# GpSimd's element-wise work moved to VectorE in a two-block fp32 transformer kernel on Trainium2

## The chip, the cores and the metric

The kernel runs on one core of a Trainium2 chip. The metric is device time in microseconds for one execution; a version's time is the median of its runs. One execution more was recorded by the hardware profiler, and all rows below are from it. The engines are PE (TensorE: matrix products), DVE (VectorE: element-wise work), ACT (ScalarE: functions, scaled copies), POOL (GpSimd: here also element-wise work) and SP (transfers only).

## The reference

Two transformer blocks run one after the other on 512 rows of width 1024, all in fp32. The first is two layers of swiglu, a mixer (Fourier mix, dilated-window attention, differential attention) and a second swiglu. The second block is where most of the change lies:

```python
h = _rms_norm(x, g_mix_pre[l])
proj = h @ w_in[l]
aq, ak, av, dqkv, dgate, dalpha, dbeta = jnp.split(proj, IN_SPLITS, axis=-1)
...
attn_o = _window_attention(aq, ak, av, attn_sink[l]).astype(x.dtype)
dn_o = _gated_deltanet(dqkv, dgate, dalpha, dbeta, conv_w[l], a_log[l], dt_bias[l],
                       g_dn_out[l]).astype(x.dtype)
mix = jnp.concatenate([attn_o, dn_o], axis=-1) @ w_out[l]
x = x + _rms_norm(mix, g_mix_post[l])
c = _memory_cross_attention(_rms_norm(x, g_cross_pre[l]), _rms_norm(mem, g_mem[l]),
                            w_cq[l], w_ckv[l], w_co[l])
x = x + _rms_norm(c, g_cross_post[l])
f = _swiglu(_rms_norm(x, g_ffn_pre[l]), w_gate_up[l], w_down[l])
x = x + _rms_norm(f, g_ffn_post[l])
```

The gated deltanet takes queries, keys and values through a convolution of five taps, a silu and a norm, and then runs a recurrence over chunks, in both directions and for four heads.

## The kernel before

**Products.** Every large product is made of three: each operand is split into a high part (rounded to fp32r) and a low part (the rest), and high x high, high x low and low x high are summed. A weight slab is loaded by SP into `raw` (3 buffers); ACT writes the high part `whi` (5 buffers), and a subtraction writes the low part `wlo` (5 buffers). `split` does the subtraction on DVE. `split_w` is the same, but while `pool_w` is set (from the second block's mixer to the end of its cross attention) every second subtraction runs on POOL.

**Order of the work.** The program is written by tasks (Python generators) that `drive` runs by priority. Each recorded operation passes through `note`, which keeps an estimate of when each engine is free and when each tile is done; a task yields until the tile that it needs is due, and others are written in between. So an engine's order is fixed when the program is built, and an operation that moves to another engine changes the due times and with them the order of everything behind it. Work of low priority fills what would be waits: the gates and window projections, and `memory_proj` (priority 7), which multiplies the memory rows by K and V weights and sends six of its results to DRAM through POOL's queue.

**What POOL does before.** In the first block: the running sums of squares (`sq_pool`, L471), seven additions per norm. At the start of the second block's mixer: eight scalings of x by its norm (`final_norm`, L1258). In the mixer: four additions in each convolution of queries and values (`conv`), half of the weight splits, copies and products in `delta_k`; in `delta` the masks times beta and the scalings of values, keys and queries; and in `rope` the sine product and the sum. In the norms between mixer, cross attention and swiglu (`post_task`, `post_halves`): the odd chunks' scaling and sums. At the end: the gain of the last norm (`finish`). Fills (memset) and transfers too.

The convolution on POOL's path (queries, values) before: ACT makes three scaled copies, POOL adds two of them with a shift, DVE adds two taps, POOL adds the sum.

```python
if pool:
    zs = [self.g(), self.g()]
    for z, j in zip(zs, (0, 4)):
        nc.scalar.activation(z, t, AF.Copy, scale=wc(j))
    yield self.when(*zs)
    nc.gpsimd.tensor_tensor(zs[0][:, 0:S - 4], zs[0][:, 0:S - 4], zs[1][:, 4:S], ALU.add)
```

Of the kernel before, what the change touches and what calls it, by code (L numbers as in the profile page):

```python
# [135 lines left out]
class Net:  # L136
    def __init__(self, ctx, tc, ins, dump=None):
# [21 lines left out]
        self.pool_w = self.turn = False  # L159
# [146 lines left out]
    def split_w(self, src, hi, lo):  # L306

        self.nc.scalar.activation(hi, src, AF.Copy)
        self.turn = self.pool_w and not self.turn
        (self.nc.gpsimd if self.turn else self.nc.vector).tensor_tensor(lo, src, hi.bitcast(F32), ALU.subtract)  # L310
        return hi, lo

# [4 lines left out]
    def slab(self, src, kc, c, whole=False):  # L317
# [142 lines left out]
    def sq_pool(self, k, x):  # L460
# [9 lines left out]
        else:  # L470
            nc.gpsimd.tensor_tensor(self.acc[k], self.acc[k], q, ALU.add)  # L471

    def wide(self, srcs, us, first=4):
# [4 lines left out]
        for k in range(KC):  # L478
            if k % 4 == 0:
                self.lock, self.ahead = self.cur, True  # L480
                n = first if k == 0 else 4
                for j, src in enumerate(srcs):
# [5 lines left out]
                    for c in range(2):  # L488
                        hi = self.whi.tile([P, 4, P], F32R, tag="whi", name=self.nm("whi"))
                        lo = self.wlo.tile([P, 4, P], F32R, tag="wlo", name=self.nm("wlo"))  # L490
                        for k0 in range(0, 4, n):
                            self.split_w(raw[:, k0:k0 + n, c * P:(c + 1) * P], hi[:, k0:k0 + n], lo[:, k0:k0 + n])
# [744 lines left out]
    def final_norm(self, a1, a2):  # L1237
# [19 lines left out]
        for c in range(KC):  # L1257
            nc.gpsimd.tensor_tensor(self.x[c], self.x[c], r1b, ALU.mult)  # L1258
# [5 lines left out]
    def post_task(self, row, res, nxt, done):  # L1264
# [13 lines left out]
        for c in range(1, KC, 2):  # L1278
            nc.gpsimd.tensor_tensor(ms[c], ms[c], rb, ALU.mult)
# [55 lines left out]
    def post_halves(self, row, res, nxt, half, done):  # L1335
# [22 lines left out]
        def chunks(n, cs, p=None):  # L1358
            sl = slice(256 * n, 256 * n + 256)
            for c in cs:  # L1360
                if c % 2:
                    nc.gpsimd.tensor_tensor(ms[c][:, sl], ms[c][:, sl], rbs[n], ALU.mult)
            for c in cs:
# [14 lines left out]
                else:  # L1378
                    q = self.g(shape=[P, 256])
                    nc.scalar.activation(q, x, AF.Square)  # L1380
                    eng = nc.vector if c % 2 and n else nc.gpsimd
                    eng.tensor_tensor(self.acc[0][:, sl], self.acc[0][:, sl], q, ALU.add)
# [13 lines left out]
    def wide_halves(self, srcs):  # L1396
# [5 lines left out]
        for k in range(0, KC, 4):  # L1402
            w.append([])
            for j, src in enumerate(srcs):
# [3 lines left out]
                for c in range(2):  # L1408
# [5 lines left out]
                    w[-1].append(self.split_w(raw[:, :, c * P:(c + 1) * P], hi, lo))  # L1414
# [28 lines left out]
    def mixer2_task(self, after):  # L1443
# [4 lines left out]
        self.pool_w = True  # L1448
# [15 lines left out]
        def conv(p, x, h):  # L1464
# [8 lines left out]
            pool = x != 1  # L1473
            if pool:
                zs = [self.g(), self.g()]
                for z, j in zip(zs, (0, 4)):
                    nc.scalar.activation(z, t, AF.Copy, scale=wc(j))
                yield self.when(*zs)
                nc.gpsimd.tensor_tensor(zs[0][:, 0:S - 4], zs[0][:, 0:S - 4], zs[1][:, 4:S], ALU.add)
            yield self.when(y)  # L1480
            for j in (1, 3) if pool else (0, 1, 3, 4):
# [4 lines left out]
            if pool:  # L1486

                yield self.when(zs[0])
                nc.gpsimd.tensor_tensor(y[:, 2:S], y[:, 2:S], zs[0][:, 0:S - 2], ALU.add)
                nc.gpsimd.tensor_tensor(y[:, 0:2], y[:, 0:2], zs[1][:, 2:4], ALU.add)  # L1490
                yield self.when(y)
# [57 lines left out]
        self.pool_w = True  # L1549
# [124 lines left out]
    def delta_k(self, h, st):  # L1674
# [22 lines left out]
        for d in range(2):  # L1697
# [13 lines left out]
            nc.gpsimd.tensor_copy(self.kgs[c], v3(dt)[:, :, last])  # L1711
            self.dt[c] = dt
            lt = self.g()
            (nc.vector if d else nc.gpsimd).tensor_tensor(lt, dt, kkm, ALU.mult)
# [83 lines left out]
    def delta(self, h, d, oa, done, st):  # L1798
# [69 lines left out]
        nc.gpsimd.tensor_tensor(v3(rv), v3(rv), be3, ALU.mult)  # L1868
        nc.gpsimd.tensor_tensor(v3(kg), v3(kg), self.b3(self.kgs[c]), ALU.mult)
# [11 lines left out]
        nc.gpsimd.tensor_tensor(qgt, qgt, gq, ALU.mult)  # L1881
# [56 lines left out]
    def rope(self, t):  # L1938
# [8 lines left out]
        nc.gpsimd.tensor_tensor(o, o, self.sin, ALU.mult)  # L1947
        yield self.when(o)
        nc.gpsimd.tensor_tensor(t, t, o, ALU.add)
# [202 lines left out]
    def cross_task(self, after):  # L2152
# [53 lines left out]
        self.pool_w = False  # L2206
# [64 lines left out]
    def post_gain(self, gb):  # L2271
        nc, i = self.nc, self.i
        yield 100.0
        for h in range(2):
            nc.scalar.dma_start(gb[h], i["g_ffn_post_2"][0, h * S:(h + 1) * S].partition_broadcast(P))
            nc.gpsimd.tensor_scalar_mul(gb[h], gb[h], D ** 0.5)
# [61 lines left out]
    def finish(self, t, ps, ms, xn, gb, out):  # L2338
        nc = self.nc
        ss = self.small(2, "mss")  # L2340
        for h in range(2):
# [3 lines left out]
            nc.gpsimd.tensor_tensor(ms[h], ms[h], gb[h], ALU.mult)  # L2345
# [110 lines left out]
```

## Time and profile before

| what | value |
|---|---|
| median of 3 runs | 3448.17 us (3446.51 to 3451.38) |
| profiled execution, its own time | 3459.29 us |
| its span | 3457.5 us, 44625 instructions |
| PE busy | 3356.0 us (97%) |
| DVE busy | 1905.8 us (55%) |
| ACT busy | 1369.1 us (40%) |
| POOL busy | 337.6 us (10%) |
| mean granted clock of PE | 0.986 |

A busy time is the union of an engine's instructions. The granted clock is 1 when PE runs at 2.4 GHz and 0.5 at 1.2 GHz. The second block's mixer and cross attention lie between about 2506 and 3112 us.

### The profile page before, as it was taken

How to read it: one execution, taken by the hardware profiler on the slowest of the kernel's cores; microseconds unless marked ns; L12 is line 12 of the kernel's file. 1: busy time of each engine (PE TensorE's matmuls, PEld its weight loads, DVE VectorE, ACT ScalarE, POOL GpSimd, SP SyncE). 2: the span in 40 equal slices, each digit the busy share in tenths (PEclk: the TensorE clock that was granted, in tenths of full speed). 3: DMA queues.
4: the chain of work that ended last, by engine and by line, in shares of the span. 5: the costliest groups of instructions: out<-in, count | busy, mean ns of one | idle time of the engine just before them, and what ended most of it. 6: DMA issues, size and time to landing. Idle time of an engine off the chain costs nothing.

```text
span 3457.5 us, 44625 instructions
## 1 busy us (share of the span) xinstructions
PE 3356.0 (97%) x16759; PEld 2835.2 (82%) x16759; DVE 1905.8 (55%) x3644; ACT 1369.1 (40%) x2672; POOL 337.6 (10%) x325
## 2 busy tenths in 40 slices
PE   8999999999999999999999999999978889999998
PEld 7788888898888888888888987888867887788887
DVE  5444476656444444444767474545488764754344
ACT  4323445543332333234445443333354443443232
POOL 1000100000000000001000001000354433220001
PEclk9999999999999999999999999999999999999999
DMA  4533333435333333334333257333336453223232
GB/s 123 151 104 101 117 96 101 124 109 176 93 95 101 95 100 90 100 96 121 96 101 119 86 189 147 102 102 96 93 121 189 152 156 107 68 74 99 96 98 85
DMA packets 424422, 386.46 MB, mean 112 GB/s; under 512 B 31184, under 2 KB 379577, under 8 KB 424205
## 3 DMA queue, kind: packets, MB, share of 16 engines
q1 hardware_dynamic: 383584, 333.50, 32.2%
q10 hardware_dynamic: 40141, 48.54, 5.2%
q8 instruction: 131, 2.15, 0.3%
q0 software_dynamic: 480, 1.57, 0.1%
q14 instruction: 86, 0.70, 0.1%
HBM read 341.46 MB, written 37.88 MB: 110 GB/s over the span
## 4 chain that ended last, share of the span: by engine, by line
PE 90%; DVE 5%; DMA 2%; ACT 1%; issue 1%; POOL 0%; SPq 0%; ACTq 0%; DVEq 0%; POOLq 0%
PE ps L119 90%; DVE g L119 3%; DVE sm L119 1%; ACT g L119 1%; DVE wlo L119 0%; DMA raw<-in_w_ffn_gate 0%; ACT whi L119 0%; DVE tmp L119 0%; DMA g<-xinv_d 0%; DMA raw<-in_w_in 0%; DMA raw<-in_w_ffn_up 0%; DMA g<-cs_d 0%; ACT L119 0%; DMA g<-in_g_ffn 0%; DMA g<-in_x 0%
## 5 line engine op out<-in xcount | busy, mean ns | idle before, releaser
L119 PE MATMUL ps<-g,whi 128*128 128x512 f32 (+1 forms) x7776 | 2396.9, 390 | 19.7 <-ACT g L119 9.4
L119 PEld LDWEIGHTS ps<-g,whi 128*128 128x128 f32 x7776 | 1450.3, 189 | 314.1 <-ACT g L119 11.1
L119 PE MATMUL ps<-g,wlo 128*128 128x512 f32 (+1 forms) x3888 | 1508.6, 388 | 4.7 <-DVE wlo L119 2.8
L119 ACT ACTIVATE whi<-raw 128x512 fp32r<-128x512 f32 (+2 forms) x1100 | 673.0, 617 | 1347.2 <-PE ps L119 1216.8
L119 DVE TENSOR_TENSOR wlo<-raw,whi 128x512 fp32r<-128x512 f32 (+2 forms) x1038 | 706.3, 685 | 607.6 <-ACT whi L119 589.2
L119 PEld LDWEIGHTS ps<-g,wlo 128*128 128x128 f32 x3888 | 735.6, 189 | 157.2 <-DVE wlo L119 4.9
L119 DVE TENSOR_TENSOR g<-ps,g 128x512 f32<-128x512 f32 (+3 forms) x486 | 299.1, 625 | 422.9 <-PE ps L119 342.4
L119 DVE TENSOR_TENSOR g<-g,g 128x512 f32<-128x512 f32 (+3 forms) x494 | 352.9, 726 | 133.3 <-ACT g L119 124.7
L119 POOL TENSOR_TENSOR g<-g,g 128x512 f32<-128x512 f32 (+4 forms) x142 | 181.9, 1289 | 2142.7 <-ACT g L119 2088.8
L119 ACT ACTIVATE g<-g 128x512 fp32r<-128x512 f32 (+3 forms) x473 | 289.8, 617 | 206.3 <-DVE g L119 171.5
L119 PE MATMUL ps<-g,g 128*128 128x128 f32 (+6 forms) x1638 | 265.7, 310 | 19.0 <-ACT g L119 7.1
L119 PE MATMUL ps<-whi,g 128*128 128x256 f32 (+1 forms) x1184 | 259.2, 312 | 0.0
L119 PEld LDWEIGHTS ps<-g,g 128*128 128x128 f32 (+3 forms) x1638 | 224.2, 193 | 40.2 <-ACT g L119 8.5
L119 PEld LDWEIGHTS ps<-whi,g 128*128 128x128 f32 x1184 | 198.0, 193 | 11.4
L119 PE MATMUL ps<-wlo,g 128*128 128x256 f32 (+1 forms) x592 | 183.9, 311 | 0.0
L119 ACT ACTIVATE g<-ps 128x256 fp32r<-128x256 f32 (+6 forms) x231 | 95.6, 426 | 150.5 <-PE ps L119 128.2
L119 DVE SCALAR_TENSOR_TENSOR g<-ps,g 128x512 f32<-128x512 f32 x114 | 83.5, 734 | 103.7 <-PE ps L119 101.7
L119 PEld LDWEIGHTS ps<-wlo,g 128*128 128x128 f32 x592 | 114.3, 193 | 5.9
L119 POOL TENSOR_TENSOR wlo<-raw,whi 128x512 fp32r<-128x512 f32 x62 | 86.5, 1396 | 222.0 <-ACT whi L119 198.0
L119 ACT COPY g<-ps 128x512 f32<-128x512 f32 (+6 forms) x154 | 59.5, 417 | 111.2 <-PE ps L119 106.1
L119 ACT ACTIVATE g<-g,sm 128x512 f32<-128x512 f32 (+3 forms) x160 | 89.0, 579 | 31.2 <-DVE sm L119 28.3
L119 PE MATMUL ps<-ident,g 128*128 128x128 f32 (+1 forms) x491 | 79.1, 286 | 21.4 <-DVE g L119 12.2
(173 smaller groups left out, 1352.4 us busy)
## 6 DMA issues: line engine op xcount, KB each, us to landing
raw<-in_w_ffn_gate SPq DMA_DIRECT2D x87, 512.0 KB
raw<-in_w_ffn_up SPq DMA_DIRECT2D x87, 512.0 KB
raw<-in_w_in SPq DMA_DIRECT2D x80, 512.0 KB
raw<-in_w_ffn_down SPq DMA_DIRECT2D x64, 512.0 KB
raw<-in_w_gate SPq DMA_DIRECT2D x48, 512.0 KB
raw<-in_w_gate_up SPq DMA_DIRECT2D x44, 512.0 KB
raw<-in_w_ffn_down SPq DMA_DIRECT2D x64, 192.0 KB
gd<-g ACTq DMA_DIRECT2D x48, 256.0 KB
```

What stands on the lines that cost most here:

```text
L119: r = f(*a, **k)
```

## The change

All element-wise work of POOL goes to DVE; POOL keeps fills and transfers. `split_w` and its switch are gone, so all low parts are made on DVE. The convolutions of queries and values take the form that those of keys had: one scaled copy on ACT and four multiply-adds on DVE. Everywhere else `nc.gpsimd` becomes `nc.vector` at the same place in the program. The core of the diff:

```diff
-    def split_w(self, src, hi, lo):
-
-        self.nc.scalar.activation(hi, src, AF.Copy)
-        self.turn = self.pool_w and not self.turn
-        (self.nc.gpsimd if self.turn else self.nc.vector).tensor_tensor(lo, src, hi.bitcast(F32), ALU.subtract)
-        return hi, lo
...
-            self.split_w(q[4], hi, lo)
+            self.split(q[4], hi, lo)
...
-            nc.gpsimd.tensor_tensor(self.acc[k], self.acc[k], q, ALU.add)
+            nc.vector.tensor_tensor(self.acc[k], self.acc[k], q, ALU.add)
...
-            nc.gpsimd.tensor_tensor(self.x[c], self.x[c], r1b, ALU.mult)
+            nc.vector.tensor_tensor(self.x[c], self.x[c], r1b, ALU.mult)
...
-            nc.gpsimd.tensor_tensor(ms[c], ms[c], rb, ALU.mult)
+            nc.vector.tensor_tensor(ms[c], ms[c], rb, ALU.mult)
...
-            pool = x != 1
-            if pool:
...
-            for j in (1, 3) if pool else (0, 1, 3, 4):
+            for j in (0, 1, 3, 4):
...
-            nc.gpsimd.tensor_tensor(v3(bm[lev]), mk.unsqueeze(1).to_broadcast([P, NT, P]), be3, ALU.mult)
+            nc.vector.tensor_tensor(v3(bm[lev]), mk.unsqueeze(1).to_broadcast([P, NT, P]), be3, ALU.mult)
...
-        nc.gpsimd.tensor_tensor(v3(rv), v3(rv), be3, ALU.mult)
-        nc.gpsimd.tensor_tensor(v3(kg), v3(kg), self.b3(self.kgs[c]), ALU.mult)
+        nc.vector.tensor_tensor(v3(rv), v3(rv), be3, ALU.mult)
+        nc.vector.tensor_tensor(v3(kg), v3(kg), self.b3(self.kgs[c]), ALU.mult)
...
-        nc.gpsimd.tensor_tensor(qgt, qgt, gq, ALU.mult)
+        nc.vector.tensor_tensor(qgt, qgt, gq, ALU.mult)
...
-        nc.gpsimd.tensor_tensor(o, o, self.sin, ALU.mult)
+        nc.vector.tensor_tensor(o, o, self.sin, ALU.mult)
...
-            nc.gpsimd.tensor_tensor(ms[h], ms[h], gb[h], ALU.mult)
+            nc.vector.tensor_tensor(ms[h], ms[h], gb[h], ALU.mult)
```

What this does to the order, at three places. A row names the operation and the tiles, with buffer numbers.

**First place: DVE at the start of the second mixer.** `g4553` is the first key head times the norm (`mul_rb`), `par` marks a tap of a convolution, and g3841 to g3848 are the chunks of x. Before:

```order
L119 TENSOR_TENSOR g4553_21468<-ps4512_21231,g4539_21349 128x512
L119 TENSOR_TENSOR wlo4566_21507<-raw4562_21500,whi4565_21506 128x512
L119 TENSOR_TENSOR g4555_21478<-ps4513_21232,g4539_21349 128x512
L119 SCALAR_TENSOR_TENSOR g4554_21470<-g4553_21468,par_773,g4554_21470 128x510
L119 SCALAR_TENSOR_TENSOR g4554_21470<-g4553_21468,par_773,g4554_21470 128x511
```

With the change:

```order
L119 TENSOR_TENSOR g4553_21468<-ps4512_21231,g4549_21381 128x512
L119 TENSOR_TENSOR g3841_17973<-g3841_17973,g4551_21424 128x512
...
L119 TENSOR_TENSOR g3848_17987<-g3848_17987,g4551_21424 128x512
L119 TENSOR_TENSOR g4554_21470<-ps4513_21232,g4549_21381 128x512
L119 TENSOR_TENSOR g4569_21525<-ps4514_21233,g4549_21381 128x512
L119 TENSOR_TENSOR g4570_21527<-ps4515_21234,g4549_21381 128x512
L119 TENSOR_TENSOR ab_21220<-ps4567_21501,sm4537_21318 128x64
L119 SCALAR_TENSOR_TENSOR g4568_21506<-g4553_21468,par_773,g4568_21506 128x510
```

Eight scalings of x now stand ahead of the first tap; they were on POOL.

**Second place: PE behind the small projection `ab`** (`abl` is its last row). A row with `ident` transposes a finished key head. Before:

```order
L119 MATMUL ps4552_21443<-g4509_21207,abl_21217 16x512
L119 MATMUL ps4557_21482<-ident_102,g4554_21470 128x128 x4
L119 MATMUL ps4571_21518<-g4418_20774,whi4563_21502 128x512
```

With the change:

```order
L119 MATMUL ps4552_21443<-g4509_21207,abl_21217 16x512
L119 MATMUL ps4565_21492<-g4418_20774,whi4557_21476 128x512
...
L119 MATMUL ps4573_21555<-g4496_21145,wlo4564_21489 128x512
L119 MATMUL ps4580_21606<-ident_102,g4568_21506 128x128 x4
L119 MATMUL ps4573_21555<-g4509_21207,whi4563_21488 128x512
L119 MATMUL ps4573_21555<-g4510_21208,whi4563_21488 128x512
L119 MATMUL ps4584_21622<-ident_102,g4571_21539 128x128 x4
```

The first transpose stood right behind `abl`; now 45 large products of the next slab stand between them.

**Third place: PE in the deltanet's scan** (`vw` and `st` are the scan's values and states; `vdh` and `vdl` belong to the window attention; products of 128x256 with `whi` or `wlo` are `memory_proj`). Before, K and V products stand among the scan's:

```order
L119 MATMUL ps5042_23687<-vw5043_23690,g4954_23346 128x128
L119 MATMUL ps5072_23790<-g4942_23300,g5021_23578 64x64 x4
L119 MATMUL ps5058_23724<-g3928_18346,whi5051_23711 128x256
L119 MATMUL ps5058_23724<-g3929_18347,whi5051_23711 128x256
L119 MATMUL ps5058_23724<-g3928_18346,wlo5052_23712 128x256
```

With the change the last of them, and a stretch of the scan some 230 rows later:

```order
L119 MATMUL ps4843_22909<-wlo4836_22865,g3928_18346 128x256
L119 MATMUL ps4843_22909<-whi4835_22864,g3929_18347 128x256
L119 MATMUL ps4844_22935<-ident_102,g4780_22603 128x128 x4
...
L119 MATMUL ps5056_23869<-g5044_23833,vdh1_23269 128x512
L119 MATMUL ps5056_23869<-g5045_23834,vdh1_23269 128x512
L119 MATMUL ps5035_23805<-g4966_23530,st5027_23772 128x128
L119 MATMUL ps5035_23805<-g5010_23700,vw5036_23808 128x128
L119 MATMUL ps5056_23869<-g5044_23833,vdl1_23270 128x512
L119 MATMUL ps5038_23815<-g5033_23800,vw5039_23817 128x128
```

All of the first six K and V slabs (288 products) now stand ahead of the scan's first product; before, 48 did, and 240 were spread over the scan.

## Rows read from the trace of the kernel before

**Rows 1.** The page, busy time by engine: us (share of span) xinstructions.

```profile
PE 3356.0 (97%) x16759; PEld 2835.2 (82%) x16759; DVE 1905.8 (55%) x3644; ACT 1369.1 (40%) x2672; POOL 337.6 (10%) x325
```

**Rows 2.** Windows: stretch, its length, busy PE, PEld, DVE, ACT, POOL; PEclk, DMA, GB/s.

```profile
864.40:950.80 86.40, 86.40 (x391) 71.77 (x390) 42.20 (x72) 33.30 (x53) 6.47 (x5) 1.00 0.33 93
2506.00:2660.00 154.00, 126.84 (x618) 102.18 (x618) 139.44 (x274) 78.00 (x202) 79.14 (x68) 0.92 0.49 148
2660.00:2900.00 240.00, 216.26 (x1535) 197.79 (x1534) 154.67 (x387) 99.40 (x252) 83.38 (x70) 0.95 0.49 148
2900.00:2960.00 60.00, 50.01 (x232) 40.89 (x231) 38.74 (x47) 26.66 (x47) 28.05 (x19) 0.89 0.30 97
3064.00:3112.00 48.00, 42.93 (x301) 41.50 (x301) 38.32 (x90) 25.87 (x59) 15.83 (x18) 0.89 0.22 67
```

**Rows 3.** Waits of PE, 2506 to 2660: us in total, times, longest.

```profile
PE ps L119 <- ACT g L119: 14.2, 4, 6.1
PE ps L119 <- DVE g L119: 9.6, 1, 9.6
```

**Rows 4.** Groups by form: DVE from 1296 to 1550, then POOL from 2506 to 3112.

```profile
L119 DVE TENSOR_TENSOR wlo<-raw,whi 128x512 fp32r<-128x512 f32 x86 | 59.1, 687 | 56.3 <-ACT whi L119 54.3 <-PE ps L119 2.0
...
L119 POOL TENSOR_TENSOR wlo<-raw,whi 128x512 fp32r<-128x512 f32 x57 | 79.5, 1397 | 211.9 <-ACT whi L119 194.9 <-PE ps L119 16.9
```

**Rows 5.** Timeline 2507 to 2530, DVE and POOL: start, us, what, count.

```profile
2510.85 11.29 DVE L119 SCALAR_TENSOR_TENSOR g<-g,par,g 128x510 f32<-128x510 f32 x7
2522.06 1.75 DVE L119 TENSOR_TENSOR wlo<-raw,whi 128x512 fp32r<-128x512 f32 x1
...
2525.40 0.74 DVE L119 SCALAR_TENSOR_TENSOR g<-g,par,g 128x510 f32<-128x510 f32 x1
...
2508.48 13.11 POOL L119 TENSOR_TENSOR g<-g,g 128x512 f32<-128x512 f32 x8 [8.48 <-ACT g L119]
```

**Rows 6.** Timeline of PE at the longest wait; below it the window behind.

```profile
2525.62 1.08 PE L119 MATMUL ps<-ident,g 128*128 128x128 f32 x4 [9.57 <-DVE g L119]
...
2526.00:2531.00 5.00, 5.00 (x15) 4.03 (x14) 2.27 (x6) 2.10 (x10) 0.00 (x0) 0.50 0.39 131
```

**Rows 7.** Groups by form, PE, 2660 to 2900: the K and V products.

```profile
L119 PE MATMUL ps<-whi,g 128*128 128x256 f32 x96 | 18.8, 288 | 0.0
L119 PE MATMUL ps<-g,whi 128*128 128x256 f32 x64 | 14.4, 320 | 0.0
...
L119 PE MATMUL ps<-wlo,g 128*128 128x256 f32 x48 | 13.6, 283 | 0.0
...
L119 PE MATMUL ps<-g,wlo 128*128 128x256 f32 x32 | 9.8, 306 | 0.0
```

**Rows 8.** Timeline of PE, K and V products in a row.

```profile
2926.62 0.40 PE L119 MATMUL ps<-g,whi 128*128 128x256 f32 x2
...
2927.33 0.40 PE L119 MATMUL ps<-g,whi 128*128 128x256 f32 x2
```

**Rows 9.** Waits of PE, 2660 to 2900.

```profile
PE ps L119 <- DVE st L119: 7.1, 4, 3.3
PE ps L119 <- DMA g<-xinv_d: 4.9, 2, 3.9
PE ps L119 <- DVE sm L119: 4.4, 2, 3.3
```

**Rows 10.** Groups by form, DVE, 2660 to 2900.

```profile
L119 DVE TENSOR_TENSOR wlo<-raw,whi 128x512 fp32r<-128x512 f32 x18 | 14.7, 817 | 9.5 <-ACT whi L119 8.2 <-PE ps L119 1.3
```

**Rows 11.** Window at the scan's end, with hardly a K or V product.

```profile
2840.00:2880.00 40.00, 39.90 (x315) 36.23 (x315) 22.75 (x64) 10.03 (x26) 7.09 (x6) 1.00 0.40 128
```

**Rows 12.** Timeline of DVE after the mixer's output; PE's waits, 2900 to 2960.

```profile
2928.43 6.77 DVE L119 TENSOR_TENSOR g<-g,g 128x512 f32<-128x512 f32 x4 [0.67 <-POOL g L119]
2935.13 1.75 DVE L119 SCALAR_TENSOR_TENSOR g<-g,gain,g 128x512 fp32r<-128x512 f32 x1
...
PE ps L119 <- ACT g L119: 4.8, 1, 4.8
PE ps L119 <- DVE g L119: 2.2, 1, 2.2
```

More of the change, by code (lines that the diff above doesn't have):

```diff
@@ L158, in __init__ @@
         self.lock = None
-        self.pool_w = self.turn = False
         self.mem, self.kv, self.kvs = 0, [0] * 4, {}
@@ L491, in wide @@
                         for k0 in range(0, 4, n):
-                            self.split_w(raw[:, k0:k0 + n, c * P:(c + 1) * P], hi[:, k0:k0 + n], lo[:, k0:k0 + n])
+                            self.split(raw[:, k0:k0 + n, c * P:(c + 1) * P], hi[:, k0:k0 + n], lo[:, k0:k0 + n])
                         w[2 * j + c] = hi, lo
@@ L1361, in chunks @@
                 if c % 2:
-                    nc.gpsimd.tensor_tensor(ms[c][:, sl], ms[c][:, sl], rbs[n], ALU.mult)
+                    nc.vector.tensor_tensor(ms[c][:, sl], ms[c][:, sl], rbs[n], ALU.mult)
             for c in cs:
@@ L1380, in chunks @@
                     nc.scalar.activation(q, x, AF.Square)
-                    eng = nc.vector if c % 2 and n else nc.gpsimd
-                    eng.tensor_tensor(self.acc[0][:, sl], self.acc[0][:, sl], q, ALU.add)
+                    nc.vector.tensor_tensor(self.acc[0][:, sl], self.acc[0][:, sl], q, ALU.add)
         p = yield from norm(0)
@@ L1413, in wide_halves @@
                         lo = self.wlo.tile([P, 4, P], F32R, tag="wlo", name=self.nm("wlo"))
-                    w[-1].append(self.split_w(raw[:, :, c * P:(c + 1) * P], hi, lo))
+                    w[-1].append(self.split(raw[:, :, c * P:(c + 1) * P], hi, lo))
         self.ahead = False
@@ L1447, in mixer2_task @@
         self.free = NB - 16 - 9 - 5 - self.mem
-        self.pool_w = True
         st = {"cv": {}, "str": False, "k": [False] * 4, "q": [False] * 4, "v": [False] * 4, "nt": [0, 0], "solved": [False] * 2,
@@ L1472, in conv @@
             nc.scalar.activation(y, t, AF.Copy, scale=wc(2))
-            pool = x != 1
-            if pool:
[L1475 to L1479, printed above, removed]
             yield self.when(y)
-            for j in (1, 3) if pool else (0, 1, 3, 4):
+            for j in (0, 1, 3, 4):
                 dd = j - 2
@@ L1485, in conv @@
             yield self.when(y)
[L1486 to L1491, printed above, removed]
             nc.scalar.activation(t, y, AF.Tanh, scale=0.5)
@@ L1548, in mixer2_task @@
             self.spawn(self.solve_task(half, st), 1)
-        self.pool_w = True
         for x in (0, 2):
@@ L1710, in delta_k @@
             self.kgs[c] = self.pcst([P, NT], f"kgs{c}")
-            nc.gpsimd.tensor_copy(self.kgs[c], v3(dt)[:, :, last])
+            nc.vector.tensor_copy(self.kgs[c], v3(dt)[:, :, last])
             self.dt[c] = dt
             lt = self.g()
-            (nc.vector if d else nc.gpsimd).tensor_tensor(lt, dt, kkm, ALU.mult)
+            nc.vector.tensor_tensor(lt, dt, kkm, ALU.mult)
             yield self.when(lt)
@@ L1946, in rope @@
         yield self.when(o)
-        nc.gpsimd.tensor_tensor(o, o, self.sin, ALU.mult)
+        nc.vector.tensor_tensor(o, o, self.sin, ALU.mult)
         yield self.when(o)
-        nc.gpsimd.tensor_tensor(t, t, o, ALU.add)
+        nc.vector.tensor_tensor(t, t, o, ALU.add)
         yield self.when(t)
@@ L2205, in cross_task @@
         yield from self.out_proj(i["w_co_2"][0], G_CROSSPOST, xs, res, 6, ready, half)
-        self.pool_w = False
     def cross_q(self, ps, q):
@@ L2275, in post_gain @@
             nc.scalar.dma_start(gb[h], i["g_ffn_post_2"][0, h * S:(h + 1) * S].partition_broadcast(P))
-            nc.gpsimd.tensor_scalar_mul(gb[h], gb[h], D ** 0.5)
+            nc.vector.tensor_scalar_mul(gb[h], gb[h], D ** 0.5)
     def ffn2_task(self, out):
```

## The prediction

> **What bounds the kernel now.** I read the page first, to see how much work is to move: POOL is busy 337.6 us [rows 1]. Then the windows, to see where it lies and what is full there. Outside the second block's mixer and cross attention PE never rests where POOL adds up squares: 86.40 of 86.40 us, with DVE at 42.2 (first line of [rows 2]). The change is therefore decided between 2506 and 3112 us, in three kinds of stretches [rows 2]:
>
> - The front, 2506 to 2660: projections, convolutions, norms. PE works 126.8 of 154 us and waits 27.2; DVE is busy 139.4, that is 91%. PE's waits are for tiles at the end of DVE chains: 9.6 us for one DVE tile, 14.2 for ACT tiles that DVE feeds [rows 3].
> - The scan of the deltanet with the window attention, 2660 to 2900: PE 216.3 of 240 us, DVE 154.7.
> - The norms between mixer, cross attention and swiglu, 2900 to 2960 and 3064 to 3112: 10.0 and 5.1 us of waits.
>
> **What POOL costs DVE.** The same subtraction of 128x512 takes 687 ns on DVE where POOL rests, and 1397 ns on POOL [rows 4]. But look at both engines side by side [rows 5]: while POOL runs eight scalings in 13.11 us, DVE needs 11.29 us for seven taps, 1.6 us each, and 1.75 for a subtraction; the first tap after POOL's stretch takes 0.74. Seven free taps would take 5.2 us. So 13.1 us of POOL took 6.1 us from DVE, 0.47 us for each microsecond. The eight scalings will cost DVE 8 x 0.687 = 5.5. Where both are full, the move costs DVE nothing; where DVE has idle time it costs something, and there is room.
>
> **The change part by part.** I price POOL's time on DVE as 0.687/1.397 = 0.49 of it.
>
> 1. First block, last swiglu and tail: seven additions per norm, at PE stretches without a gap. 0 us, hidden by PE's products; DVE at 42 of 86 us has room. Were that cover gone, each addition could cost its 0.7 us. I keep 0 to +2.
>
> 2. Front. To DVE come 79.1 x 0.49 = 38.9 us; 79.1 x 0.47 = 37 come back, since DVE is nearly always busy there. The refund is bounded by 0 and these 37. DVE then has 141 us of work, as much as now. ACT loses two scaled copies in each of eight convolutions; they are not awaited, 0. What changes is PE's order. The longest wait now, 9.57 us [rows 6], is a transpose right behind the small projection; behind it PE runs at half clock, 1.2 GHz [rows 6]. With the change 45 products stand ahead of that transpose, 45 x 0.221 = 9.9 us (86.4 us for 391 products [rows 2]). DVE meanwhile has eight scalings (5.5 us), four products with the norm (2.7), eight taps at 0.74 (5.9), two more tiles (1.4) and about 1 us of small ones: 16.5 us from 2508.6, plus up to 3 for a full buffer and the tanh. PE arrives at about 2526, DVE at 2525 to 2528; I leave 2 us of wait. For the other 17.6 us of waits there is now filler: the 240 K and V products that lay in the scan [rows 7] stand ahead of it. Six take 0.71 us [rows 8], so they are 28.3 us of PE work. PE: 126.8 + 28.3, less 6 us for matmuls no longer at half clock (a granted 0.92 over 126.8 us bounds that at 10) = 149. With 6 us of waits in all (2 at the transpose, 4 of the 17.6) the front takes 155 against 154: **+1**. Bounds: no wait, -5; all 17.6 left, +15.
>
> 3. Scan. PE's work falls by the same 28.3 us to 188, less 4 for half clock (0.95 granted) = 184. DVE: 154.7, plus 83.4 x 0.49 = 41, less a refund between 0 and 39. Subtractions here take 817 against 687 ns [rows 10], a slight loss, so I take 14: about 182 of 240. Now the waits. PE waits 23.7 us here, for scan states (7.1), transfers (4.9) and window sums (4.4) [rows 9], and these are latencies, with the filler present. Without it, and behind a DVE that is busier, they grow. How far the trace doesn't show; from below they stay at 24, from above I take three times that, 71. In the scan's last 40 us there is hardly any filler and PE works 39.90 of 40 [rows 11]: four chains at once can feed it, with DVE at 57%. That is nearest, but DVE will be fuller, so I take double, 47. The stretch: 184 + 47 = 231 against 240, **-9**. Bounds -32 and +15.
>
> 4. Norms between. After the mixer's output, PE waits 4.8 and 2.2 us for the first chunks [rows 12]; DVE starts at 2928.43, after POOL, does four operations in 6.77 us and the first low part until 2936.9. With the change it is four scalings, the first chunk's scaling and sum and the low part: 6 x 0.687 + 0.74 = 4.9 us from 2927.1, so 2932. The first wait ends a little earlier and the second goes: 3 us. Two of the later 3 us, behind slowed subtractions, go too: **-5**, bounds 0 and -9. In the second norm 15.8 us of POOL give DVE 7.8 us and take about as much from it: 0, give or take 2.
>
> 5. Fills and the six transfers on POOL's queue now have nothing ahead of them. Nobody waits for them: 0. What was queued on POOL now stands in DVE's order; in the front the scalings delay the first tap, which is in the sum above.
>
> Sum: +1 - 9 - 5 = -13 us. The profiled execution's span goes from 3457.5 to 3444.5. Its own time, 3459.3, is 11.1 above the median of the runs; on the median, 3448.2 - 13 = **3435 us**. That is 0.38%; what can be told from no change here begins at about 0.2%, 6.9 us.
>
> **The rivals.**
>
> The bare scan: slower. The K and V products are used up early, the scan has no filler, and DVE at over 75% makes every short step of the chains queue behind a 0.69 us tile. This decides if the scan's waits pass 61 us (the point where the sum is zero up to a microsecond), and at three times today's, 71 us, the sum is +1 + 15 - 5 = +11: 3459, and 3455 to 3472 around it. For it: waits on states and window sums are there now; DVE's small operations are in each link. Against it: the 39.90 of 40 us.
>
> Only places change: the same. The front stays bound by DVE, which has as much to do as before, and keeps its 17.6 us: +15 - 9 - 5 = +1, 3449, and 3441 to 3455 around it. For it: 91% of DVE now. Against it: the longest wait comes from an order that counted on a faster DVE, and the new order gives PE 28 us of other work.
>
> DVE's slowness isn't POOL's doing, so that the change gives nothing back: the front's DVE work would be 139.4 + 38.9 = 178 us in 154, at least +24, and with nothing gained behind it 3472. Against it stand the taps of 1.6 and 0.74 us within one convolution [rows 5]. The Trainium skill, "Perfetto Trace Analysis", section "Optimizing Scalar/DVE Operations", says that if DVE is saturated, offloading some work to Scalar or even GpSimd may make sense; taken alone that speaks against this change, and by it the front would be longer by these 24 us. The same section adds that the two share a read port, so that moving work between them might not help; rows 5 agree with that.
>
> **How the numbers follow.** The forecast, 3435 with 3414 to 3441 around it, 0.55. The bare scan 0.21, only places 0.20, no refund 0.04. The low end, 3414, is nearly the scan's waits unchanged (-9 becomes -32, and the sum -36, 3412). The high end, 3460, takes in the second case and half of the first rival. Beyond lie the rest of that rival, the last one and the tail of the forecast, together about 0.2. Faster by over 0.2% is the forecast and a little of the second case, 0.56; the same 0.20; slower 0.24.
>
> **What would show it.** The subtractions and taps on DVE at 0.69 and 0.74 us in the front; DVE's busy time between 2506 and 3112 up by some 30 to 60 us, not by 110. In the front PE's wait at the first transpose under 3 us and the waits together under 10. In the scan PE's waits up, to about 47 us, and the stretch still shorter than 240. After the mixer's output one wait of 4 to 5 us instead of 7. PE's granted clock in the front above 0.92. I am wrong if the scan's waits pass 61 us, if DVE's tiles stay slow, or if the front's waits stay above 15 us; and if PE's gapless stretches of the first block show waits, I missed the place.

## The result, and the profile after

The changed kernel takes 3413.6 us (median of 4 runs, 3407.4 to 3419.3) against 3449.8 us for the kernel before (4 runs): a ratio of 0.9895, 95% interval 0.9875 to 0.9915. A second series gave 0.9885 (0.9871 to 0.9898). The change is faster by about 36 us; 13 were forecast, and the time lies 0.4 us below the low end of the range. The profiled executions stand 44.3 us apart (3459.3 and 3415.0), since that of before was 9.5 us above its median; what follows locates the time in the profiles and takes its size from the ratios. In which stretch those 9.5 us lie the profiles can't say.

The page after, busy time by engine, to be held against [rows 1]:

```profile
PE 3342.1 (98%) x16759; PEld 2824.5 (83%) x16759; DVE 1944.2 (57%) x3887; ACT 1362.4 (40%) x2656; POOL 20.0 (1%) x74
```

POOL lost 318 us of work and DVE gained 38. PE has the same 16759 products and is busy 14 us less; the mean granted clock is 0.993 instead of 0.986.

The two programs have different orders, so stretches of equal clock time hold different work. I cut both at four events that are the same in each: the recurrence's first product (a row with `vw`), its last one, PE's wait for the first chunk behind the mixer's output, and PE's wait for the first chunk of the last swiglu. The rows are windows as in [rows 2]: stretch, length, busy PE, PEld, DVE, ACT, POOL, PEclk, DMA share, GB/s. Before:

```profile
2506.00:2704.60 198.60, 164.79 (x868) 135.25 (x867) 168.31 (x315) 91.13 (x229) 101.19 (x86) 0.93 0.56 165
2704.60:2879.60 175.00, 159.07 (x1193) 149.31 (x1194) 117.19 (x327) 77.28 (x210) 57.44 (x50) 0.94 0.44 138
2879.60:2927.90 48.30, 47.09 (x249) 39.73 (x248) 17.84 (x39) 21.08 (x38) 11.14 (x9) 1.00 0.28 88
2927.90:3070.80 142.90, 130.32 (x684) 111.28 (x684) 90.50 (x154) 66.02 (x145) 39.80 (x28) 0.94 0.25 78
3070.80:3457.50 386.70, 372.69 (x1741) 313.25 (x1740) 187.08 (x329) 131.28 (x237) 29.34 (x28) 0.98 0.29 92
```

After:

```profile
2507.50:2720.30 212.80, 198.44 (x1183) 170.74 (x1182) 190.87 (x441) 103.34 (x258) 3.81 (x8) 0.97 0.67 201
2720.30:2849.40 129.10, 117.68 (x877) 107.00 (x876) 102.73 (x320) 58.28 (x164) 0.00 (x0) 0.97 0.34 105
2849.40:2897.50 48.10, 47.23 (x250) 39.85 (x248) 21.49 (x48) 20.97 (x38) 0.00 (x0) 1.00 0.31 99
2897.50:3030.40 132.90, 126.21 (x685) 109.03 (x684) 87.27 (x183) 66.59 (x145) 0.00 (x0) 0.97 0.26 84
3030.40:3412.80 382.40, 369.64 (x1741) 310.34 (x1740) 187.56 (x357) 130.80 (x237) 0.00 (x0) 0.99 0.29 93
```

Length less busy PE is PE's waiting. In the mixer (first three rows) the length falls from 421.9 to 390.0 us: the waits from 51.0 to 26.7, and busy PE from 371.0 to 363.3 as the granted clock rises from 0.93 and 0.94 to 0.97. The first row grows by 14.2 us though it took over 240 K and V products worth 28.3, and the second falls by 45.9. The fourth row, with the norm behind the mixer and the cross attention, loses 10.0 us (5.9 of waits, 4.1 of busy time). The last, which begins with the norm ahead of the swiglu, loses 4.3. Everything before 2506 is 1.5 us longer.

PE's waits after, first up to the recurrence, then from there to the mixer's output (us in total, times, longest), to be held against [rows 3, 9]:

```profile
PE ps L119 <- ACT g L119: 7.8, 5, 2.7
PE ps L119 <- DVE g L119: 4.1, 5, 2.1
PE ps L119 <- DVE wlo L119: 1.7, 4, 0.7
PE ps L119 <- DVE gs L119: 0.8, 1, 0.8
...
PE ps L119 <- DVE vw L119: 5.5, 4, 1.9
PE ps L119 <- DVE sm L119: 2.3, 2, 1.4
PE ps L119 <- DVE g L119: 2.2, 4, 1.2
PE ps L119 <- ACT g L119: 1.4, 2, 0.8
PE ps L119 <- DVE st L119: 0.8, 2, 0.4
```

The 9.57 us wait of [rows 6] is gone (0.8 us for `gs` stands nearest to its place), and nothing in the recurrence waits longer than 1.9 us, where 3.3 and 3.9 stood in [rows 9]. The recurrence is what the prediction calls the scan, cut at its own products and not at 2660 and 2900.

### The profile page after: what moved, and what is told of

It reads as the page before. It is cut to its first block, busy times and chain, and to the rows that moved or that the text cites. A ratio compares the mean times of both kernels' runs of the same rounds, so it can differ in the third digit from the quotient of the medians.

```text
span 3412.8 us, 44382 instructions
## 1 busy us (share of the span) xinstructions
PE 3342.1 (98%) x16759; PEld 2824.5 (83%) x16759; DVE 1944.2 (57%) x3887; ACT 1362.4 (40%) x2656; POOL 20.0 (1%) x74
## 4 chain that ended last, share of the span: by engine, by line
PE 92%; DVE 4%; DMA 2%; ACT 1%; issue 0%; ACTq 0%; DVEq 0%; POOL 0%; SPq 0%; POOLq 0%
PE ps L119 92%; DVE g L119 3%; ACT g L119 1%; DMA g<-cs_d 1%; DMA raw<-in_w_ffn_gate 0%; DVE wlo L119 0%; DVE sm L119 0%; DMA raw<-in_w_ckv 0%; ACTq L119 0%; ACT whi L119 0%; DMA raw<-in_w_ffn_down 0%; DMA g<-in_g_ffn 0%; DMA raw<-in_w_in 0%; DMA nt_d<-g 0%; DMA g<-bias_d 0%
## 5 line engine op out<-in xcount | busy, mean ns | idle before, releaser
L119 PE MATMUL ps<-g,whi 128*128 128x512 f32 (+1 forms) x7776 | 2387.5, 389 | 14.4 <-ACT g L119 8.5
L119 DVE TENSOR_TENSOR wlo<-raw,whi 128x512 fp32r<-128x512 f32 (+2 forms) x1100 | 730.8, 670 | 603.2 <-ACT whi L119 592.9
L119 DVE TENSOR_TENSOR g<-g,g 128x512 f32<-128x512 f32 (+3 forms) x612 | 403.9, 672 | 133.9 <-ACT g L119 124.3
L119 PEld LDWEIGHTS ps<-g,g 128*128 128x128 f32 (+3 forms) x1638 | 221.5, 191 | 32.4 <-ACT g L119 8.1
L119 PE MATMUL ps<-ident,g 128*128 128x128 f32 x491 | 76.7, 281 | 13.7 <-DMA g<-in_g_ffn 7.6
L119 PEld LDWEIGHTS ps<-ident,g 128*128 128x128 f32 x491 | 60.1, 145 | 26.9 <-issue 10.1
L119 ACT ACTIVATE g<-g,gain 128x512 fp32r<-128x512 f32 (+1 forms) x80 | 54.1, 678 | 41.9 <-DVE g L119 41.8
```

Source lines behind the costliest of these rows:

```text
L119: r = f(*a, **k)
```

## The experiments

Two theories stood at the start. **A**: the gain is VectorE's own time; GpSimd's operations slow those beside them, and the new order is secondary. **B**: the gain is the new order. The runs of one series share a chip and the runs of the kernel before on it; these gave 3449.8 to 3458.9 us from series to series, so ratios to the kernel before are compared.

| run | what it is | ratio (95%) |
|---|---|---|
| change | first and second series | 0.9895 (0.9875 to 0.9915), 0.9885 (0.9871 to 0.9898) |
| e1 | order of the change, work on POOL (but the convolutions') | 0.9986 (0.9977 to 0.9995) |
| e2 | order of before, work on DVE | 0.9925 (0.9911 to 0.9938) |
| e3 | splits alone moved | 0.9961 (0.9948 to 0.9973) |
| e4 | all but the splits moved | 0.9951 (0.9939 to 0.9964) |
| e5 | norms without their sums moved | 0.9986 (0.9977 to 0.9995) |
| e9 | norms and sums moved | 0.9966 (0.9953 to 0.9978) |
| e12 | scalings of x, convolutions, deltanet, rope moved | 0.9997 (0.9988 to 1.0006) |
| e6 | change, K and V products held for the scan | 0.9945 (0.9932 to 0.9957) |
| e8 | change, DVE priced higher in the planner | 1.0025 (1.0016 to 1.0035) |
| e7, e11 | change, x scaled late | 0.9885 (0.9871 to 0.9898), 0.9889 (0.9874 to 0.9904) |
| e13 | change, useless POOL work behind splits | 0.9911 (0.9899 to 0.9924) |
| e14 | change, useless POOL work behind norms | 0.9929 (0.9918 to 0.9940) |
| e15 | change, useless POOL work behind nearly all (not the convolutions) | 1.0023 (1.0014 to 1.0032) |
| e16 | e15 with one input tile | 0.9934 (0.9920 to 0.9947) |

### Order and engine apart: e1 and e2

The recording helper gets a sixth handle that issues on one engine and is priced as another, so that the moved work keeps one version's order (but for a few swaps of neighbouring rows) and has the other's engine. For e1, in the change:

```diff
+        self.ghost = Engine(net, nc.gpsimd, "vector")
...
-            nc.vector.tensor_tensor(self.acc[k], self.acc[k], q, ALU.add)
+            nc.ghost.tensor_tensor(self.acc[k], self.acc[k], q, ALU.add)
```

and so for the other operations. For e2, in the kernel before:

```diff
+        self.ghost = Engine(net, nc.vector, "gpsimd")
...
-            nc.gpsimd.tensor_tensor(self.acc[k], self.acc[k], q, ALU.add)
+            nc.ghost.tensor_tensor(self.acc[k], self.acc[k], q, ALU.add)
```

Expected of e1:

> The changed kernel's order, with the operations still issued on GpSimd (the planner prices them as VectorE's); the convolutions keep the four taps on VectorE. Theory A (GpSimd's operations slow VectorE's, and the gain is VectorE's own time given back; the order is secondary): the gain goes, 3440 us or more, VectorE's subtractions in the mixer 0.8 us and more again. Theory B (the gain is the new order, with the K and V products ahead of the scan and the transposes later): 3413 to 3422 us.

Expected of e2:

> The order of before (the planner still prices the moved operations as GpSimd's, the convolutions keep their two extra copies and additions), with all of them issued on VectorE. Theory A: most of the gain is there, 3413 to 3425 us, PE's 9.6 us wait at the first key transpose under 5 us. Theory B: 3443 us or more, the waits where they were.

Measured: 3446.3 and 3427.2 us, against 3451.8 for the kernel before beside them. The engine alone gives 0.75%, 26 us, and the order alone 0.14%, 5 us. e2 stands 2 us above what A expected, and its wait at the first key transpose is 5.7 us rather than under 5. So most of the gain is the engine; order and engine together give 5 to 9 us more than their sum. In e1 the convolutions' additions have left POOL too, so its 5 us are not the order's alone. The mixer's two parts (cut at the first `vw` product and the output) in e1:

```profile
2507.50:2738.20 230.70, 201.46 (x1174) 174.60 (x1173) 189.34 (x366) 101.12 (x255) 99.43 (x84) 0.93 0.61 185
2738.20:2917.80 179.60, 166.95 (x1124) 149.51 (x1122) 109.90 (x329) 79.60 (x204) 42.00 (x36) 0.96 0.32 102
```

With the same order as the change, the front is 18 us longer (230.7 against 212.8), and DVE is just as busy in it, 189.3 against 190.9, though 99.4 us of work lie on POOL. Moving that work cost DVE 1.5 us there. In the second row it cost 14.3 (109.9 to 124.2) for 42.0 us of POOL. The durations say why. DVE's groups up to the recurrence, first e1, then the change (busy, mean ns):

```profile
L119 DVE TENSOR_TENSOR wlo<-raw,whi 128x512 fp32r<-128x512 f32 x32 | 31.1, 975 | 19.4 <-ACT whi L119 19.2
L119 DVE TENSOR_TENSOR g<-ps,g 128x512 f32<-128x512 f32 x32 | 21.0, 682 | 3.8 <-PE ps L119 3.7
L119 DVE SCALAR_TENSOR_TENSOR g<-g,par,g 128x510 f32<-128x510 f32 x24 | 20.7, 874 | 0.1
```

```profile
L119 DVE TENSOR_TENSOR wlo<-raw,whi 128x512 fp32r<-128x512 f32 x64 | 43.2, 685 | 14.1 <-ACT whi L119 13.8
L119 DVE TENSOR_TENSOR g<-ps,g 128x512 f32<-128x512 f32 x34 | 22.7, 683 | 1.8 <-PE ps L119 1.6
...
L119 DVE SCALAR_TENSOR_TENSOR g<-g,par,g 128x510 f32<-128x510 f32 x24 | 17.6, 740 | 1.1 <-ACT g L119 1.1
```

A subtraction of two SBUF tiles takes 975 ns beside POOL and 685 without; a tap 874 and 740. An operation that takes one input from PSUM takes 682 and 683: it isn't slowed.

The windows also show where order and engine need each other. First e2 up to the recurrence, then the recurrence itself in e2 and in e1:

```profile
2507.50:2696.20 188.70, 162.75 (x848) 135.59 (x846) 164.50 (x401) 90.88 (x227) 1.12 (x3) 0.91 0.60 178
2696.20:2863.30 167.10, 155.72 (x1197) 146.31 (x1197) 125.05 (x367) 76.66 (x208) 2.71 (x5) 0.96 0.45 139
```

```profile
2738.20:2869.60 131.40, 119.66 (x876) 109.63 (x875) 92.06 (x290) 58.56 (x166) 30.91 (x27) 0.95 0.34 108
```

Length less busy PE, and the K and V products (the filler) in the recurrence:

| run | order, engine | filler in the recurrence | PE waits up to it, us | PE waits in it, us |
|---|---|---|---|---|
| before | before, POOL | 240 | 33.8 | 15.9 |
| e1 | change, POOL | 0 | 29.2 | 11.7 |
| e2 | before, DVE | 240 | 26.0 | 11.4 |
| change | change, DVE | 0 | 14.4 | 11.4 |

Up to the recurrence the order alone saves 4.6 us of waits, the engine alone 7.8 and both 19.4. In the recurrence each alone saves what both save. The repeats agree: e5, whose mixer is that of before, waits 32.4 and 15.6 us, and the change's second run 13.3 and 11.6.

### The parts: e3, e4, e5, e9, e12

e3 sets `self.turn = False` in `split_w` of the kernel before; e4 puts `split_w` and its switch back into the change. e5 moves three lines of `post_task` and `post_halves`, e9 `sq_pool`'s addition as well:

```diff
-            nc.gpsimd.tensor_tensor(ms[c], ms[c], rb, ALU.mult)
+            nc.vector.tensor_tensor(ms[c], ms[c], rb, ALU.mult)
...
-                    eng = nc.vector if c % 2 and n else nc.gpsimd
+                    eng = nc.vector
...
-            nc.gpsimd.tensor_tensor(self.acc[k], self.acc[k], q, ALU.add)
+            nc.vector.tensor_tensor(self.acc[k], self.acc[k], q, ALU.add)
```

e12 moves the lines of `final_norm`, `conv`, `delta_k`, `delta` and `rope`.

> Of the change only the weight splits are moved to VectorE (62 of GpSimd's operations, 86.5 of its 338 us, a quarter). Theory A: a share of the gain like their share of GpSimd's time, about 9 us: 3441. If the splits alone are what matters (they feed PE directly): 3420 or less. Theory B says nothing about the size, since the order is a third one.

> The change without the splits: every second weight split of the second mixer and cross attention stays on GpSimd, all else is on VectorE. Theory A: about a quarter of the gain is lost, 3422 us. If the splits are what matters: 3440 or more. If the splits don't matter: 3414.

> The kernel before with only the norms between mixer, cross attention and last swiglu moved to VectorE (post_task, post_halves). Theory A, with what the stretches of the changed kernel show (10 us less in the cross attention, 5 less behind it): 15 us less than before, all of it after the mixer's output; the mixer itself unchanged. By the prediction's own term: 5 us less.

> The kernel before with the norms between the parts of the second block and all sums of squares (sq_pool) on VectorE; splits, convolutions, deltanet and rotary stay on GpSimd. The run before this moved the norms without sq_pool's additions, and the cross attention's stretch stayed at 142 us. If those additions, which stand behind every chunk of the norm on GpSimd, are what held it: the stretch falls to about 133 us, the last one stays at 374, and the whole gains 10 to 15 us: ratio 0.996 to 0.997. If the splits on GpSimd hold it: no change against the run without sq_pool, ratio 0.9985.

> The kernel before with only the scalings of x, the convolutions, deltanet's operations and rope moved to VectorE; splits, norms, sums and gains stay on GpSimd. If the parts add up (whole 36 us, splits 13.5, norms and sums 10 to 15): 8 to 12 us gained, ratio 0.9965 to 0.998, all of it before the mixer's output. If the order it gets decides instead: anything from 0.990 to 1.005, with the stretches after the mixer's output as before.

The splits alone give 0.39%, 13 us, where 9 were expected, and norms with sums 0.34%, 12, as expected. The scalings, convolutions and deltanet, the largest edit, give nothing that can be told from no change (0.03%), though 8 to 12 us were expected. Together these are 0.76%; the whole is 1.05 to 1.15%. The parts don't add up: without the splits the change gives 0.49%, so that the splits are worth 0.6% on top of the rest and 0.39% alone. So e4's 3435 us lie above the 3422 that A gave and below the 3440 for splits that are all that matters.

e5 missed: 0.14%, that is 5 us instead of 15, with the stretch behind the mixer's output still 141.9 us. The 5 us are what the prediction's own term said, but they lie elsewhere: the last stretch has 383.2 us instead of 386.7. That pointed at `sq_pool`, whose seven additions stand on POOL beside every chunk of the norm. With them moved, e9 (windows behind the mixer's output, e5 first):

```profile
2930.70:3072.60 141.90, 129.80 (x685) 111.00 (x684) 89.74 (x159) 66.18 (x145) 34.69 (x23) 0.95 0.25 79
```

```profile
2921.70:3054.80 133.10, 126.16 (x684) 108.13 (x684) 85.27 (x166) 66.07 (x145) 22.44 (x16) 0.97 0.26 84
```

The stretch is 133.1, as in the change, with 22.4 us of splits still on POOL. So the sums of squares hold 8.8 of the 10 us there. With them moved, the splits in that place hold nothing (132.7 in e4 with the splits on POOL); with them still on POOL the splits do hold some, for e3 has

```profile
2907.30:3046.10 138.80, 128.93 (x684) 110.07 (x684) 90.47 (x170) 66.13 (x145) 16.64 (x13) 0.95 0.25 80
```

### The place of the filler: e6

```diff
             self.lock = None
             yield 0
+            yield lambda: self.scan
             s = self.slab(w[:, D + o:D + o + 256], KC, 256, True)
...
         yield self.when(wt, rv, kg)
+        self.scan = True
         s = None
```

> The changed kernel, with memory_proj held after its first slab until the first recurrence starts, so that 240 K and V products lie in the scan as before. If filler decides the scan's waits (the prediction's term 3): the scan's waits fall well below the 11.4 us of the changed kernel and the front's rise. If filler only helps the front: the front's waits go from 14 us towards the 26 of the run with the order of before, the scan's stay at 10 to 12, and the time is 3420 to 3427 us. If its place is indifferent: 3411 to 3416.

72 of the 288 K and V products now stand ahead of the recurrence and 216 in it (288 and none in the change). Front, then scan:

```profile
2507.50:2703.70 196.20, 173.73 (x956) 146.24 (x955) 173.33 (x404) 84.36 (x216) 1.11 (x3) 0.93 0.60 178
2703.70:2874.00 170.30, 150.77 (x1126) 141.63 (x1124) 121.56 (x356) 77.52 (x206) 2.71 (x5) 0.94 0.40 129
```

The front's waits rise from 14.4 to 22.5 us, as expected if filler helps there. In the scan they don't fall, as the prediction's term 3 would have it, nor stay: they rise from 11.4 to 19.5. The ratio is 0.9945, some 18 us worse than the change, where 7 to 13 were expected. So in this order these products are worth more ahead of the recurrence than in it. That the filler itself makes the scan wait isn't shown, since e2 has 240 products there and waits 11.4 us. Why e6's scan waits more I haven't isolated; 8.9 us of the front's waits, just ahead of the recurrence, are for a transfer (`xinv_d`).

### The order's weight: e8, e7 and e11

e8 changes the planner's price of a DVE operation of 512 columns from 0.60 to 0.685 us, what the trace shows:

```diff
-            fix, per = {"vector": (0.065, 0.00105), "scalar": (0.17, 0.00075), "gpsimd": (0.1, 0.0027)}[kind]
+            fix, per = {"vector": (0.065, 0.00121), "scalar": (0.17, 0.00075), "gpsimd": (0.1, 0.0027)}[kind]
```

> The changed kernel, with the planner's price of a VectorE operation of 512 columns raised from 0.60 us to 0.685, which the trace shows for it. If the order is still off by wrong prices: 3403 to 3410 us. If the order matters little (theory A): 3411 to 3418.

Measured: 3468.3 us, 0.25% above the kernel before and 1.3% above the change. The order changes everywhere: PE's wait for weights at 2139.4 us in the change comes at 2158.0 here, and the mixer takes some 420 us instead of 390. The same operations on the same engines in another order thus cost more than the whole change brings, and a truer price made it worse. That the order is secondary, as A had it, holds for these two orders and not in general.

e7 takes the eight scalings of x out of the front: x goes to DRAM unscaled and is scaled when it comes back.

```diff
-            nc.vector.tensor_tensor(self.x[c], self.x[c], r1b, ALU.mult)
             nc.sync.dma_start(self.xd[c], self.x[c])
...
             nc.scalar.dma_start(self.x[c], self.xd[c])
+            nc.vector.tensor_tensor(self.x[c], self.x[c], r1b, ALU.mult)
```

> The changed kernel without the eight scalings of x at the front: x goes to DRAM unscaled together with the scale, and is scaled on VectorE when it comes back behind the scan, where VectorE is idle half the time. If VectorE's time still bounds the front: up to 5.5 us less than the change, 3408 to 3411. If the front is bound by the latency of its chains: 3412 to 3415.

The change itself beside it (e10, no edit):

> The change itself once more, beside the next run on one chip: ratio 0.9875 to 0.9915, as at first.

> The change with x scaled when it comes back, once more, beside the change itself: if it is worth what its first run suggests, its ratio lies 0.001 below that of the change (3 to 4 us); if that was the chip, the two agree within 0.0005.

The first run looked 0.1% better than the change's first series; beside the change on one chip the two agree within 0.0004 (0.9889 and 0.9885). In e11 the front is 3.1 us shorter (207.2 against 210.3 in the change's second run) and the recurrence 5.6 longer (135.3 against 129.7). No run beat the change.

### Slow results or a slowed VectorE: e13, e14, e15, e16

A left two ways open. POOL's work may slow DVE's beside it (A1), or POOL's own results, 1.4 us instead of 0.69, may come late (A2). The change keeps its order (DVE's rows are the same one for one, and PE's but for four), and POOL gets work whose results nobody uses:

```diff
+    def shadow(self, x):
+        if self.scr is None:
+            self.scr = self.cst([P, S], "scr")
+        n = math.prod(x.shape[1:])
+        self.nc.nc.gpsimd.tensor_tensor(self.scr[:, 0:n], x, x, ALU.mult)
...
             nc.vector.tensor_tensor(self.acc[k], self.acc[k], q, ALU.add)
+            self.shadow(q)
```

e13 has it behind every second split of the second mixer and cross attention, e14 behind the norms' scalings and sums, e15 behind both and the scalings of x, deltanet's and rope's operations; e16 is e15 with `tensor_scalar_mul(scr, x, 0.5)`.

> The changed kernel, every engine's order row for row the same, and GpSimd given useless work: after every second weight split in the mixer and cross attention it squares the finished low part into a scratch tile that nobody reads. Nobody waits for GpSimd's results. If GpSimd costs time by slowing VectorE (A1): the time rises as where the splits themselves are on GpSimd, to a ratio of 0.993 to 0.996. If it costs time because its own results come late, 1.4 us instead of 0.69 (A2): the ratio of the change, 0.988 to 0.990.

> The same with useless work behind the norms' scalings and sums of squares (post_task, post_halves, sq_pool), in the unchanged order. A1: the stretch of the cross attention goes from 133 us back towards 142, the ratio to 0.991 to 0.993. A2 (the chain of additions on GpSimd was what PE waited for): the stretch stays at 133, the ratio at 0.988 to 0.990.

> Both, and useless work behind the scalings of x, deltanet's and rope's operations too: about all of GpSimd's operations of before but the convolutions', with no result of them used. A1: the gain goes as in the run with the new order on GpSimd, a ratio of 0.996 to 1.000. A2: 0.988 to 0.990.

> The full shadow with another operation: GpSimd multiplies the same tile by a constant (one input tile) where it multiplied two; order and places are the same. If any busy GpSimd slows VectorE: ratio 0.998 to 1.003, as with two inputs, scaled with its busy time. If it is the two inputs from SBUF that collide: 0.988 to 0.991, the subtractions in the mixer at 0.69 us.

e15 takes the whole gain back and more: 1.0023, where the change has 0.9885 to 0.9895 and 0.996 to 1.000 was expected, without one result of POOL being used. That it lies above e1 fits: e1 takes the work off DVE, e15 leaves it there. Its windows from the mixer's start to the end:

```profile
2507.50:2739.80 232.30, 204.09 (x1173) 174.62 (x1171) 218.15 (x437) 100.69 (x253) 85.61 (x68) 0.93 0.60 184
2739.80:2929.90 190.10, 171.25 (x1122) 152.69 (x1122) 133.10 (x370) 80.16 (x206) 43.71 (x39) 0.95 0.32 97
2929.90:3072.20 142.30, 128.88 (x685) 110.30 (x684) 100.84 (x182) 66.82 (x145) 39.38 (x30) 0.95 0.24 78
3072.20:3459.50 387.30, 371.02 (x1741) 310.56 (x1740) 193.86 (x357) 130.78 (x237) 13.98 (x18) 0.99 0.28 91
```

Against the change they are 19.5, 12.9, 9.4 and 4.9 us longer. DVE's busy time grows in all four (in the first from 190.9 to 218.2) by the same instructions, and the granted clock falls back to 0.93 and 0.95. Even the smallest operations show it. Two of 32 columns, behind the small projection (start, us), in the change and in e15:

```profile
2519.20 0.18 DVE L119 TENSOR_TENSOR z<-ab,dtb 128x32 f32<-128x32 f32 x1
...
2520.50 0.18 DVE L119 TENSOR_SCALAR z<-z 128x32 f32<-128x32 f32 x1 [0.36 <-ACT ez L119]
```

```profile
2522.19 1.03 DVE L119 TENSOR_TENSOR z<-ab,dtb 128x32 f32<-128x32 f32 x1
...
2524.76 1.01 DVE L119 TENSOR_SCALAR z<-z 128x32 f32<-128x32 f32 x1
```

Both lie in the chain to `gs`, and PE's wait for `gs` goes from 0.8 to 6.7 us. So A1 is shown for all the work together. For the norms it holds as well: e14's two stretches behind the mixer's output are

```profile
2900.60:3042.30 141.70, 128.36 (x684) 110.09 (x684) 95.14 (x183) 66.41 (x145) 16.95 (x12) 0.95 0.24 79
3042.30:3430.40 388.10, 372.02 (x1740) 311.97 (x1740) 193.74 (x357) 130.78 (x237) 13.89 (x18) 0.98 0.28 91
```

that is 8.8 and 5.7 us longer than in the change, together all of the 14.3 that the change had won there. For the splits it is weaker. e13 loses some 0.2%, above the range for A2 (0.990) but below that for A1 (0.993), while e4, with the splits really on POOL, loses 0.6%. So for the splits the slowing accounts for about a third of their worth, roughly, since e13's interval overlaps that of the change's first series; the rest is POOL's own late results or e4's order, which the runs don't separate.

e16 falls between: 0.9934, less than half of e15's loss though POOL is busy longer (110.4 us in the front against 85.6). Its subtractions are at 719 ns up to the recurrence against 737 in e15. A reservation holds for both: the useless work keeps tiles in use, and DVE waits for it 5.6 us in e16 and 1.9 in e15.

## Why the prediction was wrong

The way was right, and with it one mechanism: POOL's work takes DVE's time, so moving it is nearly free where DVE is full. A second one was wrong, that the scan waits more when its filler leaves, and it made the size: -13 us by the sum against about -36.

**DVE's work in the mixer.** The prediction had 37 of 38.9 us come back in the front and 14 of 41 in the scan. With the order held (e1 against the change) the front's DVE time rose by 1.5 us for 99.4 us of POOL and the later part's by 14.3 for 42.0, by the price of 0.49 a refund of 47 of 49 and of 6 of 21. The two shares held, 97% and 30% where it had 95% and 34%. The amount didn't: over the mixer DVE grew by 11.7 us instead of 29, and up to the last swiglu by 8.5, not the 30 to 60 that were to be seen.

**The step that failed: "I take double, 47".** Term 3 let PE's waits in the scan grow from 23.7 to 47 us because the filler leaves. With 6 in the front that made 53 us of waits in the mixer; the trace has 26.7, about half of the 51.0 before. From 2660 to the mixer's output it has 16.4 where the sum had 47, and this lies below the term's own lower bound, 24. The waits are 26 of the 32 us that the profiles miss the sum by (by the medians it is missed by 23). Rows 11 had it right: 40 us with hardly a filler product and PE busy in 39.90. After the change the recurrence runs from 2720.3 to 2849.4 without a K or V product, and PE is busy 117.7 of 129.1 us, 91%; before, with 240 of them in it, 159.1 of 175.0, 91% too. e1 answers the term directly: no filler, GpSimd still beside VectorE, and 11.7 us of waits in the recurrence, fewer than the 15.9 of before. So the four chains and the window attention feed PE by themselves. That faster DVE tiles cut these waits isn't shown as the only cause: e1 has the order alone and e2 the engine alone, and each waits about as little as the change. Which of the waits in [rows 9] each removes stays open; one of the two longest there, 3.9 us, was for a transfer. The estimate that carried the sum was a factor between two bounds, and it went against the nearest row.

That the measured 3413.6 us lie close to the 3412 that the prediction gave for unchanged scan waits is chance: terms that were off in both directions, and a profile of before that lay 9.5 us above its median, add up to it.

**The front.** Forecast +1 us up to 2660 with 6 us of waits; the trace has 10.3 us up to there and 14.4 up to the recurrence (33.8 before). The first transposes no longer wait and the 240 products stand there, as the order said. The order alone doesn't do it: e1 has the same products there and 29.2 us of waits. Nor does the engine: e6 and e2, with fewer of them in the front, have 22.5 and 26.0.

**The norms.** Forecast -5; measured -10.0 behind the mixer's output and -4.3 ahead of the last swiglu, where the prediction had 0. Behind the output the waits alone fell by 5.9 us, from 12.6 to 6.7, so the term's number is nearly right, and so is its first wait (4.3 us, the second gone). That is luck in part: the term gave the 5 us to the scalings and the splits, but e5 moves the scalings and keeps 12.1 us of waits, while e9, with the sums of squares moved too and the splits still on POOL, has 6.9. Left out was busy PE, which fell by 4.1 and 3.1 us in the two stretches at a granted clock of 0.97 and 0.99 instead of 0.94 and 0.98. The sum had counted what the clock gives back in the mixer only.

**First block, fills, transfers.** Forecast 0, measured +1.5 up to 2506.

**The rivals.** The bare scan needed over 61 us of waits in the scan; there are 12. Only the places changed would have kept 17.6 us in the front; 10.3 are left up to 2660. That DVE's slowness isn't POOL's doing is refuted by e15. The sentence of the Trainium skill, "Perfetto Trace Analysis", section "Optimizing Scalar/DVE Operations", that a saturated DVE might offload to GpSimd doesn't fit e2: there the same order is 0.75% faster with the work on DVE, at 87% load in the front (164.5 of 188.7 us). The warning behind it, of the shared port, agrees with e15.

## What to carry to other kernels

Before work is given to a slow engine to relieve a fast one, look at the fast engine's durations while the slow one runs: here 99 us of GpSimd work saved VectorE 1.5 us. Give the second engine work that nobody uses, in an unchanged order, and its true price shows. Run the new order and the new engine each alone: here they needed each other ahead of the recurrence, 4.6 and 7.8 us of waits saved alone and 19.4 together. And where a factor has to be chosen for waits that the trace doesn't show, take the row that comes nearest, not the middle of the bounds.

## What the runs showed of the hardware that I had not expected

That GpSimd slows VectorE was in the profile before; its selectivity was not. Subtractions of two SBUF tiles took 975 ns in e1's front and 685 in the change's, operations with one input from PSUM 682 and 683. A 32-column operation took 1.03 us instead of 0.18 in e15: a small operation can lose some 0.85 us, and a chain of them loses it more than once. One of these reads a single tile from SBUF (`TENSOR_SCALAR`, 1.01 us instead of 0.18), so two inputs are not a condition. The Trainium skill, "SBUF — State Buffer", section "SBUF: two separate sides", describes it as a port pair that one of the two holds for a whole instruction, when VectorE reads two SBUF inputs and GpSimd reads SBUF, or when VectorE works in a mode that uses two ports. The 975 against 682 ns agree with that; in which mode the operation with one input ran, no run shows. A GpSimd operation with one input tile isn't free either: e16 loses 0.4 to 0.5%, and it is busy longer than e15's square, which reads one tile twice (110.4 against 85.6 us in the front).
